# A hybrid decoder layer on one core: the opening rebuilt around a transposed x

## The chip, the cores and the metric

The kernel runs on one core of one Trainium2 chip. The core has a tensor engine (PE, with its weight loads listed as PEld), a vector engine (DVE), a scalar engine (ACT), GpSimd (POOL) and SyncE (SP), which issues nearly all DMAs here. The metric is the device time of one execution in microseconds; lower is better.

## The reference, cut to what matters

One layer is computed for a prompt of 1024 tokens and a group of 8 x 8 sample tokens, 1088 tokens of width 1024 together. Only the first steps matter for this change:

```python
shift, scale, gate = split(silu(c) @ ada_w + ada_b, 3)      # one set for the prompt, one for each of 8 samples
h = rmsnorm(x, norm_w) * (1 + scale) + shift
q_lat, kv_lat, k_pe, g_a, u, g_b, m_a, m_b = split_in(h @ w_in)
...
x = x + gate * (merged @ w_out)
```

`rmsnorm` divides each token by the root of the mean of its 1024 squares. `u` (512 columns) feeds a causal convolution and a recurrence; the other columns feed latent attention (prompt and paged sample attention), gates and mixers. `gate` is needed only at the end.

## The kernel before, in words

Tokens are cut into three groups, `GRP = [(0, 364), (364, 362), (726, 362)]`; the last holds the 64 sample tokens. The 1024 features are `KC = 8` chunks of 128. A product in high precision is three f32r products (`mm3`: high by high, high by low, low by high), so each operand is split by `split` into a rounded copy (ACT) and the remainder (DVE).

The opening is the block with the pools `p1`, `pj1`, `pt1`, `px1`. PE's instructions there keep the order of the program; those of the other engines and of the DMA queue are placed by a planner, which also moves an instruction ahead of earlier ones if its inputs are there.

- `x_load` brings nine tiles of 128 tokens by 1024 features. `x_norm` sums a tile's squares on ACT, takes the power -0.5 on GpSimd (`rms_pow`) and scales the tile on DVE or GpSimd. `x_turn` turns it on PE (eight transposes) and copies it out of PSUM to `xT`, feature by token.
- `ada_load`, `ada_sum`, `ada_turn` make shift and scale of one feature chunk: a 1 MB load (`aw`), eight products with 32 columns of weights that use four column strips of PE, a copy (`sa`), two transposes (`padt`), then three small DVE instructions that leave `aff`.
- `h_part` makes h of one chunk and group: an affine instruction on GpSimd (two DVE instructions for the samples), then `split` into `hh` and `hl`.
- `u_part` multiplies a chunk into the first two column tiles of `u`: six f32r products for one group, 18 for a chunk. The loop over k runs `u_part` for chunk k, and between its groups `ada_turn` and `h_part` of chunk k + 1 and `ada_sum` of chunk k + 2.

Then `u_evac` copies the u tiles to `L[0]` and `L[1]`, whose buffers the split u weights held.

After the opening, `dense` runs through 24 further column tiles of `w_in` (`project`: 24 products of three for a tile and group). `interleave` and `sample_attention` mix it with the recurrence and with sample attention by a clock `clk` that adds up estimated PE times. In its sixteen tiles from the third on, `beside` also carries one turn of `gate_sums`: a load of 256 KB, four f32 products with 32 columns of weights (`pada`), and a copy or add into `sgs`, the tile that holds the gate's partial sums until the last stage.

## Time and profile before

| | us |
|---|---|
| median of 3 runs (lowest to highest) | 973.25 (972.82 to 973.26) |
| the profiled execution | 971.41 |
| its span | 969.6 |
| PE busy in the span | 936.1 |
| first u product starts | 28.32 |
| first projection of `dense` starts | 66.41 |

The span runs from the first instruction to the last, and lies 1.8 us under the profiled execution's own time. Times in the trace count from the span's start. PE's busy time counts pipelined products that overlap, so pitches (start to start) say more than durations.

### The profile page before, as it was taken

To read this page: it belongs to the slowest core of one execution; us is meant where nothing else is said; L and a number is where in the kernel's file an instruction comes from. 1 tells how busy PE (TensorE), PEld (TensorE's weight loads), DVE (VectorE), ACT (ScalarE), POOL (GpSimd) and SP (SyncE) were. 2 spreads that over 40 slices of the span, in tenths; PEclk is the share of its full clock that TensorE was granted. 3 is DMA by queue.
4 is the path that set the end of the run, shared out by engine and by line. 5 is a ranking of instruction groups with operands and counts; after the bars stand their busy time and mean duration, and the time that the engine had idled before them with its cause. 6 is when DMAs were issued, how large, how long until landed. Compare 5 with 4: busy or idle time off the path is not lost. (4 is left out here: it accounts for less than half of the span.)

```text
span 969.6 us, 16493 instructions
## 1 busy us (share of the span) xinstructions
PE 936.1 (97%) x5933; PEld 860.2 (89%) x5933; DVE 645.5 (67%) x1518; ACT 492.2 (51%) x1150; POOL 241.0 (25%) x313
## 2 busy tenths in 40 slices
PE   5899999999999999999999999999999899999997
PEld 4677999999999999999999898888888799998886
DVE  5775664566666777766654367889889785880833
ACT  6447555544445444544443336777687664650311
POOL 5452210332222322222100034444445200000101
PEclk9999999999999999999999999999999999999999
DMA  9843132453443323333422213000011264741421
GB/s 337 287 142 110 49 108 94 146 152 109 141 129 125 113 77 120 103 110 119 117 78 97 65 53 69 12 7 22 7 34 34 69 198 155 246 140 35 152 87 66
DMA packets 52099, 104.62 MB, mean 108 GB/s; under 512 B 8177, under 2 KB 23601, under 8 KB 50994
## 3 DMA queue, kind: packets, MB, share of 16 engines
q1 hardware_dynamic: 46626, 84.69, 26.8%
q0 software_dynamic: 5392, 18.88, 6.6%
q8 instruction: 47, 0.77, 0.3%
q14 instruction: 34, 0.28, 0.1%
HBM read 85.58 MB, written 16.92 MB: 106 GB/s over the span
## 5 line engine op out<-in xcount | busy, mean ns | idle before, releaser
L79 PE MATMUL pj<-hh,whi 128*128 128x362 f32 (+2 forms) x656 | 223.9, 341 | 1.1 <-ACT L L145 1.1
L81 PE MATMUL pj<-hh,wlo 128*128 128x362 f32 (+2 forms) x656 | 217.1, 331 | 0.0
L80 PE MATMUL pj<-hl,whi 128*128 128x362 f32 (+2 forms) x656 | 216.8, 330 | 0.0
L79 PEld LDWEIGHTS pj<-hh,whi 128*128 128x128 f32 x656 | 123.5, 188 | 7.5 <-issue 4.7
L80 PEld LDWEIGHTS pj<-hl,whi 128*128 128x128 f32 x656 | 123.7, 189 | 1.7 <-issue 0.4
L81 PEld LDWEIGHTS pj<-hh,wlo 128*128 128x128 f32 x656 | 123.4, 188 | 1.7 <-issue 0.4
L644 POOL TENSOR_SCALAR nat<-raw 128x1024 fp32r<-128x1024 f32 x32 | 37.0, 1157 | 136.6 <-PE spo L65 81.6
L1038 POOL TENSOR_SCALAR pr<-pr,mx 128x128 f32<-128x128 f32 (+3 forms) x64 | 50.0, 782 | 83.2 <-DVE mx L1037 69.3
L1036 ACT ACTIVATE pr<-pr,mx 128x128 f32<-128x128 f32 (+3 forms) x64 | 49.8, 778 | 12.9 <-DVE mx L1034 12.6
L645 DVE TENSOR_TENSOR nat<-raw,nat 128x1024 fp32r<-128x1024 f32 x32 | 39.0, 1220 | 20.6 <-POOL nat L644 20.6
L641 POOL DMA_INDIRECT raw<-cache_ckv,idx x32 | 33.6, 1049 | 74.9 <-PE ptt L69 44.4
L1052 PE MATMUL ptr<-ident,pr 128*128 128x128 f32 x288 | 45.6, 276 | 4.1 <-DVE ptl L56 2.7
L112 POOL TENSOR_SCALAR ost<-ost 128x1 f32<-128x1 f32 (+1 forms) x9 | 2.9, 324 | 186.0 <-DVE ost L1296 186.0
L1293 ACT ACTIVATE ot<-xo 128x512 f32<-128x512 f32 (+2 forms) x19 | 11.5, 606 | 72.8 <-DVE xo L1292 68.5
L56 DVE TENSOR_TENSOR ptl<-ptr,pth 128x512 fp32r<-128x512 f32 (+1 forms) x80 | 45.7, 577 | 3.6 <-ACT pth L55 2.4
L694 ACT COPY stmp<-pss 64x512 f32<-64x512 f32 (+1 forms) x40 | 19.9, 497 | 55.0 <-PE pss L65 54.7
L56 DVE TENSOR_TENSOR wlo<-wraw,whi 128x512 fp32r<-128x512 f32 x58 | 39.4, 703 | 10.1 <-ACT whi L55 10.0
L55 ACT CAST pth<-ptr 128x512 fp32r<-128x512 f32 (+1 forms) x80 | 39.6, 499 | 9.7 <-PE ptr L1052 9.1
L56 DVE TENSOR_TENSOR tt<-ptt,tt 128x512 fp32r<-128x512 f32 x64 | 41.2, 679 | 4.8 <-ACT tt L55 4.4
L1052 PEld LDWEIGHTS ptr<-ident,pr 128*128 128x128 f32 x288 | 33.0, 140 | 12.6 <-DVE ptl L56 3.9
L55 ACT CAST whi<-wraw 128x512 fp32r<-128x512 f32 x58 | 34.0, 621 | 13.5 <-PE pj L80 13.4
L345 DVE COPY ev<-pj 128x364 f32<-128x364 f32 (+1 forms) x40 | 21.2, 530 | 29.4 <-PE pj L81 28.9
(472 smaller groups left out, 2588.5 us busy)
## 6 DMA issues: line engine op xcount, KB each, us to landing
wraw<-w_in SPq DMA_DIRECT2D x60, 256.0 KB, 3.2
sg<-g_dram SPq DMA_DIRECT2D x16, 544.0 KB, 3.6
aw<-ada_ss SPq DMA_DIRECT2D x8, 1024.0 KB, 7.2
g_dram<-ev SPq DMA_DIRECT2D x40, 181.0 KB, 2.4
wraw<-ada_g SPq DMA_DIRECT2D x16, 256.0 KB, 3.0
oraw<-w_out SPq DMA_DIRECT2D x16, 256.0 KB, 3.2
xo<-xp SPq DMA_DIRECT2D x8, 512.0 KB, 5.3
out_y<-xo SPq DMA_DIRECT2D x16, 256.0 KB, 2.1
```

The costliest lines, as they stand in the source:

```text
L55: S.copy(hi, src)
L56: V.tensor_tensor(lo, src, f(hi), OP.subtract)
L79: T.matmul(out, lhs[0], rhs[0], start=start, stop=False)
L80: T.matmul(out, lhs[0], rhs[1], start=False, stop=False)
L81: T.matmul(out, lhs[1], rhs[0], start=False, stop=stop)
L345: (S.copy if g == 1 else V.tensor_copy)(ev[:, :n], ps[:, :n])
L641: nc.gpsimd.indirect_dma_start(raw.rearrange("p k r -> p (k r)"), None, ckv_rows, bass.IndirectOffsetOnAxis(ap=idx[:, j, b:b + 1], axis=0))
L644: G.tensor_scalar(nat[:, 0], raw, 1.0, 0.0, OP.mult, OP.add)
L645: V.tensor_tensor(nat[:, 1], raw, f(nat[:, 0]), OP.subtract)
L1036: S.activation(pr[:, :w], pr[:, :w], AF.Exp, bias=mx[:, 1:2], scale=-1.0, accum_out=mx[:, 2:3])
L1038: G.tensor_scalar(pr[:, :w], pr[:, :w], mx[:, 3:4], 0.0, OP.mult, OP.add)
L1052: T.transpose(ps[:, k, i, :], pr[i][:, kc * P:(kc + 1) * P], ident)
```

## The change: what it does

The host now also lays x out feature by token, as three arrays `xT0` to `xT2`, one for each token group. `x_load` brings each in two halves of four chunks. The squares are taken on ACT, chunk by chunk; DVE (groups 0 and 1) or GpSimd (group 2) adds the eight up; PE sums over the partitions with a column of ones; the power is taken for three columns at once; three diagonal tiles and a product with a matrix of ones spread the result over all partitions (`R`). DVE then scales x in place: the first two chunks in the opening, the others in `h_part`, where the sample instructions go to GpSimd. Eight warm-up products of the identity stand ahead of the first modulation sum. The loop turns the modulation two blocks ahead instead of one, and has four buffers `aw` instead of three. The gate's sums use `ada_sum` on four loads of 1 MB: two in the last blocks, two at the end of the opening. `gate_sums` and its turns in `beside` are removed. The diff, cut to its core:

```diff
-        G.tensor_tensor(out, tmp, nhalf[:n], OP.pow)
+        G.tensor_tensor(out, tmp, nhalf[:n].to_broadcast(tuple(out.shape)), OP.pow)
...
-            xT = p1.tile([P, KC, N], F32, name="xT", bufs=1)
+            xg = [p1.tile([P, KC, n], F32, name=f"xT{g}", bufs=1) for g, (_, n) in enumerate(GRP)]
+            ones = p1.tile([P, P], F32, name="ones", bufs=1)
+            V.memset(ones, 1.0)
             def ada_load(k):
-                aw = p1.tile([P, KC, 256], F32, name="aw", bufs=3)
-                nc.sync.dma_start(aw, a["ada_ss"][k])
+                aw = p1.tile([P, KC, 256], F32, name="aw", bufs=4)
+                nc.sync.dma_start(aw, a["ada_ss"][k] if k < KC else a["ada_g"][k - KC])
...
+            def x_load(g):
                 for j in range(2):
+                    nc.sync.dma_start(xg[g][:, 4 * j:4 * j + 4], a[f"xT{g}"][:, 4 * j:4 * j + 4])
+            def x_sum(g):
+                n = GRP[g][1]
+                acc = p1.tile([P, 364], F32, name="acc", bufs=3)
+                S.activation(acc[:, :n], xg[g][:, 0], AF.Square)
+                for k in range(1, KC):
+                    sq = p1.tile([P, 364], F32, name="sq", bufs=3)
+                    S.activation(sq[:, :n], xg[g][:, k], AF.Square)
+                    (V if g < 2 else G).tensor_tensor(acc[:, :n], acc[:, :n], sq[:, :n], OP.add)
+                return acc
+            def x_turn(g, acc):
+                pq = px.tile([P, 4], F32, name="pst", tag="px")
+                for i, m in cut[g]:
+                    T.matmul(pq[:m, i:i + 1], acc[:, i * P:i * P + m], ones[:, 0:1], start=True, stop=True)
...
+                V.tensor_copy(st[g][:, 0:2], pq[:, 0:2])
+                V.tensor_copy(st[g][:m, 2:3], pq[:m, 2:3])
+                rms_pow(st[g][:, 4:7], st[g][:, 0:3], D, st[g][:, 0:3])
+            def x_spread(g):
+                rinv = p1.tile([P, 3, P], F32, name="rinv", bufs=2)
+                for i in range(3):
+                    V.tensor_scalar(rinv[:, i], ident, st[g][:, 4 + i:5 + i], None, OP.mult)
+                ps = pt.tile([P, 512], F32, name="prb", tag="pt")
+                T.matmul(ps[:, :n], ones, rinv.rearrange("p i t -> p (i t)")[:, :n], start=True, stop=True)
+                R[g] = p1.tile([P, 364], F32, name=f"R{g}", bufs=1)
+                S.copy(R[g][:, :n], ps[:, :n])
+            def x_scale(g, k, m):
+                x = xg[g][:, k:k + m]
+                V.tensor_tensor(x, x, R[g][:, :n].rearrange("p t -> p () t").to_broadcast((P, m, n)), OP.mult)
             def h_part(k, g):
...
+                if k > 1:
+                    x_scale(g, k, 1)
                 if s + n > NP:
...
-                    V.tensor_tensor(h3, xT[:, k, NP:]..., OP.mult)
-                    V.tensor_tensor(h3, h3, aff[:, k, 0, 1:9]..., OP.add)
+                    G.tensor_tensor(h3, x3, aff[:, k, 1, 1:9]..., OP.mult)
+                    G.tensor_tensor(h3, h3, aff[:, k, 0, 1:9]..., OP.add)
                     split(hh[k][:, NP:], hl[k][:, NP:], hs[:, k])
+                G.tensor_scalar(h[:, s:m], x[:, :m - s], aff[:, k, 1, 0:1], aff[:, k, 0, 0:1], OP.mult, OP.add)
                 split(hh[k][:, s:m], hl[k][:, s:m], h[:, s:m])
+            def gate_sum(j):
+                return ada_sum(aw[KC + j], sgs[:, 256 * j:256 * j + 256])
...
+            for g in range(3):
+                x_load(g)
+            aw = {0: ada_load(0)}
+            u01 = [weights(a["w_in"][c], (0,), (w_u0, None)[c]) for c in range(2)]
+            aw[1], aw[2] = ada_load(1), ada_load(2)
+            for c in range(2):
+                weights(a["w_in"][c], (1,), u01[c])
+            aw[3] = ada_load(3)
+            for g in range(3):
+                x_turn(g, x_sum(g))
+                x_spread(g)
+                x_scale(g, 0, 2)
+            warm = px.tile([P, P], F32, name="warm", tag="px")
             for i in range(8):
+                T.matmul(warm, ident, ident, start=i == 0, stop=i == 7)
+            sa = ada_sum(aw[0])
+            aw[4] = ada_load(4)
+            ada_turn(0, sa)
+            for g in range(3):
+                h_part(0, g)
+            sa = ada_sum(aw[1])
+            aw[5] = ada_load(5)
+            def block_sum(k):
+                if k < KC:
+                    r = ada_sum(aw[k])
+                elif k < KC + 2:
+                    r = gate_sum(k - KC)
+                if k + 4 < KC + 4:
+                    aw[k + 4] = ada_load(k + 4)
+                return r
+            def block_turn(k, sa):
+                if k < KC:
+                    ada_turn(k, sa)
+                    for g in range(3):
+                        h_part(k, g)
             for k in range(KC):
                 if k == 3:
                     w_u2 = weights(a["w_in"][2])
+                u_part(k, 0)
+                if k == 0:
+                    block_turn(1, sa)
+                    u_part(0, 1)
+                    sa = block_sum(2)
+                    u_part(0, 2)
+                    block_turn(2, sa)
+                else:
+                    sa = block_sum(k + 2)
+                    u_part(k, 1)
+                    block_turn(k + 2, sa)
+                    u_part(k, 2)
+            gate_sum(2)
+            gate_sum(3)
+            nc.sync.dma_start(sgs[9:10], a["gate_b"])
...
             def beside(n):
                 w[n + 1] = weights(a["w_in"][tiles[n + 1][0] if n + 1 < len(tiles) else 8])
-                m = n - 2
-                sums = gate_sums(m // 2, m % 2) if 0 <= m < 16 else iter(())
-                next(sums, None)
-                yield
-                next(sums, None)
                 yield
```

## Rows read from the trace of the kernel before

**Rows 1.** The page, busy time, share and instructions of each engine.

```profile
PE 936.1 (97%) x5933; PEld 860.2 (89%) x5933; DVE 645.5 (67%) x1518; ACT 492.2 (51%) x1150; POOL 241.0 (25%) x313
```

**Rows 2.** Windows of the opening: length, busy time by engine, PE's clock, DMA, GB/s.

```profile
10.00:12.00 2.00, 2.00 (x10) 1.64 (x9) 0.15 (x1) 1.77 (x4) 1.74 (x4) 1.00 1.03 422
...
30.00:31.00 1.00, 1.00 (x6) 0.92 (x5) 0.41 (x2) 0.60 (x3) 0.00 (x0) 0.50 0.70 279
...
33.00:34.00 1.00, 1.00 (x18) 0.50 (x11) 1.00 (x3) 0.66 (x2) 1.00 (x1) 1.00 0.10 41
```

**Rows 3.** Timeline from 7 to 18 us: start, length, instruction, idle before it.

```profile
7.49 0.21 POOL L532 COPY L<-vec 128x24 f32<-128x24 f32 x1
...
8.74 1.06 ACT L224 ACTIVATE L<-x 128x1024 f32<-128x1024 f32 x1 [0.32 <-DMA x<-xp]
...
9.04 6.99 PE L238 MATMUL pxt<-ident,x 128*128 128x128 f32 x32 [9.04 <-DVE x L229]
...
14.59 0.19 POOL L112 TENSOR_SCALAR st<-st 128x1 f32<-128x1 f32 x1
...
14.86 0.55 POOL L113 TENSOR_TENSOR st<-st,nhalf 128x1 f32<-128x1 f32 x1
...
16.34 1.07 PE L238 MATMUL pxt<-ident,x 128*128 128x128 f32 x8 [0.31 <-DVE x L229]
```

**Rows 4.** Timeline of PE in the u stage and into the first projection.

```profile
28.32 0.43 PE L79 MATMUL pu<-hh,wuh 128*128 128x364 f32 x1 [2.38 <-ACT hh L55]
...
40.21 0.33 PE L81 MATMUL pu<-hh,wlo 128*128 128x364 f32 x1
40.38 0.39 PE L202 MATMUL padt<-ident,sa 128*128 128x128 f32 x2
...
40.77 0.33 PE L80 MATMUL pu<-hl,wuh 128*128 128x362 f32 x1
...
41.43 0.32 PE L81 MATMUL pu<-hh,wlo 128*128 128x362 f32 x1
41.69 1.07 PE L194 MATMUL pada<-aw,sc 128*32 128x256 f32 x16
...
42.96 0.33 PE L80 MATMUL pu<-hl,wuh 128*128 128x362 f32 x1
...
59.13 0.38 PE L202 MATMUL padt<-ident,sa 128*128 128x128 f32 x2
...
61.70 0.43 PE L79 MATMUL pu<-hh,wuh 128*128 128x364 f32 x1 [0.20 <-ACT hh L55]
...
66.41 0.43 PE L79 MATMUL pj<-hh,whi 128*128 128x364 f32 x1 [1.06 <-ACT L L145]
```

**Rows 5.** PE around the first gate turn; then all turns of that tile.

```profile
118.94 0.33 PE L81 MATMUL pj<-hh,wlo 128*128 128x362 f32 x1
119.20 0.42 PE L65 MATMUL pada<-wraw,sc 128*32 128x128 f32 x8
...
119.83 0.33 PE L80 MATMUL pj<-hl,whi 128*128 128x362 f32 x1
...
L65 PE MATMUL pada<-wraw,sc x128: 272/285/297, 119.2 to 385.2; 128*32 128x128 f32 x128
```

**Rows 6.** GpSimd's instructions by shape: count, busy time, mean ns, idle before.

```profile
L937 POOL TENSOR_TENSOR csr<-csr,sq 128x512 f32<-128x512 f32 x2 | 2.6, 1280 | 64.4 <-ACT sq L908 64.4
...
L1295 POOL TENSOR_TENSOR xo<-xo,gain 128x256 f32<-128x256 f32 x1 | 0.7, 739 | 0.9 <-ACT ot L1293 0.9
```

**Rows 7.** Timelines of GpSimd and DVE in one block of the u stage.

```profile
42.36 0.64 POOL L245 TENSOR_SCALAR L<-xT,aff 128x362 f32<-128x362 f32 x1
42.93 0.54 DVE L56 TENSOR_TENSOR hl<-L,hh 128x364 fp32r<-128x364 f32 x1 [0.91 <-ACT hh L55]
42.99 0.95 POOL L245 TENSOR_SCALAR L<-xT,aff 128x298 f32<-128x298 f32 x1
```

**Rows 8.** Timeline of PE at a product in plain f32 (ones by squares).

```profile
567.93 1.02 PE L938 MATMUL qss<-csr,ones 128*128 128x512 f32 x2
```

More of the change, by code (lines that the diff above doesn't have):

```diff
@@ L194, in ada_sum @@
                     T.matmul(ps[32 * t:32 * t + 32, :], sc[:, j, :], aw[:, j, :], start=j < 4, stop=j >= 4)
-                sa = p1.tile([P, 256], F32, name="sa")
+                sa = p1.tile([P, 256], F32, name="sa") if sa is None else sa
                 S.copy(sa, ps)
@@ L231, in x_turn @@
-            def x_turn(i):
-                n, x = P if i < 8 else NS, xs[i]
-                for j in range(2):
-                    ps, tag = ((pt, "pt"), (pj, "pj"), (pj, "pj"))[(2 * i + j) % 3]
-                    ps = ps.tile([P, 4, P], F32, name="pxt", tag=tag)
-                    for k in range(4):
-                        T.transpose(ps[:, k, :n], x[:n, (4 * j + k) * P:(4 * j + k + 1) * P], ident[:n, :n])
-                    (S.copy if j == 0 and i % 2 == 0 else V.tensor_copy)(xT[:, 4 * j:4 * j + 4, i * P:i * P + n], ps[:, :, :n])
@@ L255, in trunk_step, with u_part @@
             pu = {}
[L257 removed]
+            def u_part(k, g):
                 s, n = GRP[g]
[L259 to L279 removed]
@@ L280, in trunk_step @@
-            aw = ada_load(2)
-            h_part(0, *GRP[0])
-            h_part(0, *GRP[1])
-            h_part(0, *GRP[2])
-            sa = ada_sum(aw1)
-            for k in range(KC):
-                if 0 < k and k + 2 < KC:
-                    aw = ada_load(k + 2)
-                if k == 0:
-                    for c in range(2):
-                        weights(a["w_in"][c], (1,), u01[c])
+                for c in range(2):
+                    if k == 0:
+                        pu[c, g] = (pj if g < 2 else pt).tile([P, 512], F32, name=f"pu{c}{g}",
+                                                             tag="pj" if g < 2 else "pt")
+                    mm3(pu[c, g][:, :n], [w[:, k, :] for w in u01[c]], [hh[k][:, s:s + n], hl[k][:, s:s + n]],
+                        k == 0, k == KC - 1)
@@ new lines, in trunk_step @@
+            for g in range(3):
[3 more added lines that the diff above has]
+            aw[1], aw[2] = ada_load(1), ada_load(2)
+            for c in range(2):
+                weights(a["w_in"][c], (1,), u01[c])
[5 more added lines that the diff above has]
+            warm = px.tile([P, P], F32, name="warm", tag="px")
@@ L324, in project @@
                 next(beside, None)
-        def gate_sums(k, q):
-            aw = wp.tile([P, 512], F32, name="wraw", bufs=3)
-            nc.sync.dma_start(aw.rearrange("p (k j) -> p k j", k=4), a["ada_g"][k, :, 4 * q:4 * q + 4])
-            yield
-            ps = pj.tile([P, P], F32, name="pada", tag="pj")
-            for t in range(4):
-                mm(ps[32 * t:32 * t + 32, :], sc[:, 4 * q + t, :], aw[:, P * t:P * t + P], start=True, stop=True)
-            to = sgs[:, P * k:P * k + P]
-            if q == 0:
-                V.tensor_copy(to, ps)
-            else:
-                V.tensor_tensor(to, to, ps, OP.add)
-            if k == 7 and q == 1:
-                nc.sync.dma_start(sgs[9:10], a["gate_b"])
         def spill(c):
```

75 lines of the change are left out of this document (20 added, 55 removed).

## The prediction

> **What bounds the kernel now.** The page's engine totals come first: the tensor engine (PE) is busy for 97% of the span [rows 1], so what it must execute, and when it can begin, sets the end. The windows and the timeline then divide the part that the change touches in two. From 0 to 28.3 us PE only turns x and waits; its first u product starts at 28.32, the first projection of the next stage at 66.41, and from there PE runs with few holes until the end [rows 4]. So the sum needs three numbers: when the first u product starts, how long the u stage lasts, and what the sixteen gate turns cost among the projections.
>
> The clock column belongs beside it. It stands at 0.50 (1.2 GHz) in the microsecond from 30, after 2.38 us without work ahead of 28.32, and at 1.00 (2.4 GHz) in that from 33 [rows 2, 4]. The column also says 1.00 in the first microseconds, but there 32 transposes take 6.99 us, 0.218 each, and later eight take 1.07, at most 0.134 each [rows 3]: PE starts slow there too and comes up only after several microseconds of work.
>
> **What leaves the projections.** In each of the sixteen places PE goes from the product before a gate turn to the second after it in 0.89 us (118.94 to 119.83); two ordinary products take 0.333, so a turn costs 0.555 [rows 5]. PE does not wait there, so nothing hides it: 16 x 0.555 = -8.9 us. Their copies and adds on the vector engine (DVE) and their 256 KB loads are off the path and are priced at nothing.
>
> **What the u stage becomes.** It holds 144 u products. At 2.4 GHz their pitch is 0.1665. A modulation sum put between them costs 1.53 - 0.333 = 1.197 (41.43 to 42.96), a turn 0.56 - 0.333 = 0.23 (40.21 to 40.77) [rows 4]. After the change: 144 x 0.1665 = 24.0; eight sums between products (2 to 7, and two of the gate) 9.6; seven turns 1.6; the last two gate sums back to back 2 x 1.07 = 2.1, which also cover the 1.06 that PE now waits for the evacuation before 66.41. Together 37.3. Before, the stage took 66.41 - 28.32 = 38.1, with the slow clock and some stalls in it; because the turns come a block earlier I take most stalls as gone and leave 0.7 for new ones (0 to 3): 38.0, a difference of -0.1. If the clock fell again as it did before 30 it would cost some 1.5 more.
>
> **When the first u product starts.** PE's program order is fixed, so the summed squares of the third token group, their turn, the spread, eight warm-up products and the first modulation sum all stand ahead of it. Backwards from there:
>
> - Arrival. The third x tile (1.91 MB moved, the three constant tables included) was there at 8.74, when its square began [rows 3]. The first half of the third group ends at 4.05 MB; the rest goes at 422 GB/s [rows 2]: 8.74 + 5.1 = 13.8. Two squares of 364 columns (0.38 each by columns from 1.06 for 1024 [rows 3]) and their latency put GpSimd's first add at 14.7.
> - Seven adds on GpSimd. A two-input instruction takes 1.28 at 512 columns and 0.739 at 256 [rows 6], so 0.97 at 362: 6.8 us. The second group's power stands in the same queue: 0.19 + 0.55 for one column [rows 3], 0.36 of it for the power; three columns cost between 0.85, hops included, and 1.6; I take 1.0. End without disturbance: 22.5.
> - Collisions. GpSimd needs 0.64 for 362 columns alone, but 0.95 for 298 when a two-input DVE instruction started just before it [rows 7]: 0.42 is lost by one collision (0.53 would be due). While the adds run, DVE has the eight scalings of the first group, ready as soon as its spread is: an instruction that is ready is placed early here even if its stage comes much later (the copy of line 532 at 7.49 belongs to the recurrence [rows 3]). Eight collisions: 3.4 (0 if they fall elsewhere, 5 with the weight splits and a part of the second group's scalings). End: 25.9.
> - Turn of the third group: six short passes on PE at the low clock, 0.2 each as the transposes [rows 3], 1.2; two copies 0.45; the power 1.0; three diagonal products on DVE 0.65 (0.22 each, an estimate by the columns of 0.54 for 364 [rows 7]): 3.3.
> - Spread. A product of 512 columns in plain f32 comes in two passes that take 1.02 together, 0.43 apart [rows 8], so 0.61 for 362 at 2.4 GHz. PE has done almost nothing until here, so I take 1.2 GHz: 1.25.
> - Warm-up. Eight times 128 columns are two such products: 1.7 at the high level, 3.4 at the low one. PE came up only after more than 3.4 us of work in both places that the trace shows (from 28.32 to after 31, and the transposes from 9.04), so I take 3.4.
> - First modulation sum: 1.07 at the high level [rows 4], about 1.9 at the low; 1.5. Copy from PSUM 0.45. From a turn's start to the u product that needs its features: 59.13 to 61.70, 2.57 [rows 4].
>
> 25.9 + 3.3 + 1.25 + 3.4 + 1.5 + 0.45 + 2.57 = 38.4, against 28.3: +10.1.
>
> **The sum.** -8.9 - 0.1 + 10.1 = +1.1. The profiled execution took 971.41, so 972.5 for one like it; it lies 1.84 below the median of 973.25, so 974.3 in those terms. The new opening gives back almost exactly what the projections gain. Differences within 0.2% (1.95 us) are about what a measurement of this kernel can't tell from no change.
>
> Edits at no cost: the loads of the gate weights (four of 1 MB; each is issued four sums before it is used, some 18 us by the blocks above, and takes 2.5 us at 422 GB/s [rows 2]); the two sample instructions of each block that go to GpSimd; the new layout on the host. The 72 transposes of x and their copies save nothing by themselves: they end in 28.3, which the chain above replaces.
>
> A sentence from the notes beside it: the Trainium skill (GPSIMD Engine Reference, 3.1 Elementwise) gives 4497 ns for a two-input add of 2048 columns. By that the seven adds take 5.6 us, an estimate from that page, not 6.8, and the sum would be 973.1. The trace's own rows at 256 and 512 columns are nearer in size.
>
> **Rivals.**
>
> *The start is hardly late (faster).* If the scalings fall after GpSimd's adds and the clock rises in the middle of the warm-up, 3.4 and 1.2 go away: -3.5, 969.8. For it: nothing but the order that the planner finds puts the scalings early, and the program names them only at the blocks that use them. Against it: the early copy at 7.49, and adds that run for 7 us while DVE has free time. It decides when the adds end before 22.8.
>
> *The shared port bounds the blocks (slower).* If the scalings for features 2 to 7 are not made early, each block holds on DVE three scalings and four subtractions with two inputs (about 2.6 us at 0.42 for 364 columns) and on GpSimd three affine instructions (1.8) and the two sample ones (0.3 each, between the 0.19 and 0.55 of its short instructions [rows 3]): 5.0, and 5.6 if each scaling also waits 0.2 for GpSimd as the second subtraction of a block does now. PE's block is 18 x 0.1665 + 1.2 + 0.23 = 4.4. Six blocks lose 7.1, less 1.5 of lead; the early collisions (3.4) and the 0.3 of stalls already counted go away: 1.1 + 5.6 - 3.7 = +3.0, 976.3. It becomes slower than before by more than 0.2% from 5.4 us a block on. For it: in the rows the two engines take turns rather than overlap [rows 7]. Against it: DVE has idle time between the third group's spread and the first u product, some 9 us, for just these scalings. The Trainium skill (GPSIMD Engine Reference, 1. Specifications) states that GpSimd's SBUF interface is shared with the vector engine and contended by its two-input instructions; by that rule it is this rival that happens, at 976.3, and the trace's 0.95 against 0.53 agrees.
>
> *The gain in the projections doesn't arrive.* If something else ended those stretches, only the late start would be left: 983. PE's uninterrupted pitch on both sides of each turn speaks against it.
>
> **Chances.** No change within 0.2% (971.3 to 975.2): 0.38, where the likeliest sum, 974.3, lies. Faster: 0.27, the first rival and shorter GpSimd adds. Slower: 0.35, of which the shared port 0.2, the third rival 0.02, and the upper ends (powers of three columns at 1.6 twice, +1.2; stalls up to 3; collisions up to 5) 0.13. The range takes the first rival at its lower end and the upper bounds added to the sum, +5.2: 969.5 to 979.5.
>
> **What the next profile would show.** Right: the first u product between 36 and 40; GpSimd's adds above 0.97 in the mean and ending near 26; warm-up products 0.43 apart; sums between u products at 1.2 and no `pada` among the projections; first projection 38 us after the first u product. Wrong if the adds end by 22, if the warm-up runs at the high clock from its start, if u blocks are longer than 4.6 with waits for the features, or if an engine's queue holds the third group's squares behind a copy of an earlier spread (ACT serves both), which would add up to 2 us.

## The result, and the profile after

The changed kernel takes 994.36 us (median of 4, 993.57 to 996.7), the kernel before beside it 973.04 (4 runs): a ratio of 1.0226, 95% interval 1.0213 to 1.0239. It is slower by 21 us where no change was forecast. The span is 992.7 against 969.6, so 23.1 us have to be found, of which the forecast had 1.1. Three marks on PE divide them: the first u product, the first projection, and the first product of squares behind the attention (`qss`).

| | before | forecast | after | after against forecast |
|---|---|---|---|---|
| first u product | 28.3 | 38.4 | 43.9 | +5.5 |
| length of the u stage | 38.1 | 38.0 | 48.3 | +10.3 |
| first projection to `qss` | 501.5 | 492.6 | 499.0 | +6.4 |
| from there to the end | 401.7 | 401.7 | 401.5 | -0.2 |

All three terms are off, in the same direction. PE's busy time, from the page, is what it was in [rows 1]; the time is lost in idle PE and at the low clock.

```profile
PE 934.9 (94%) x5837; PEld 859.7 (87%) x5837; DVE 649.9 (65%) x1522; ACT 493.2 (50%) x1158; POOL 241.2 (24%) x320
```

**The opening**, in timelines of ACT, DVE, GpSimd (POOL) and PE, answers to [rows 3] and [rows 6].

```profile
14.54 0.51 ACT L228 ACTIVATE sq<-xT 128x362 f32<-128x362 f32 x1 [1.77 <-DVE acc L229]
16.71 1.15 ACT L228 ACTIVATE sq<-xT 128x362 f32<-128x362 f32 x2 [1.66 <-DVE st L238]
17.90 0.46 ACT L253 COPY R<-prb 128x364 f32<-128x364 f32 x1
...
13.70 0.16 DVE L239 COPY st<-pst 128x2 f32<-128x2 f32 x1 [1.20 <-PE pst L236]
15.55 0.68 DVE L249 TENSOR_SCALAR rinv<-ident,st 128x128 f32<-128x128 f32 x3 [1.04 <-POOL st L113]
25.45 2.05 DVE L249 TENSOR_SCALAR rinv<-ident,st 128x128 f32<-128x128 f32 x3 [1.04 <-POOL st L113]
...
19.64 3.45 POOL L229 TENSOR_TENSOR acc<-acc,sq 128x362 f32<-128x362 f32 x3 [4.12 <-ACT sq L228]
24.54 0.87 POOL L113 TENSOR_TENSOR st<-st,nhalf 128x3 f32<-128x3 f32 x1
25.38 4.57 POOL L229 TENSOR_TENSOR acc<-acc,sq 128x362 f32<-128x362 f32 x4
...
30.00 1.37 PE L236 MATMUL pst<-ones,acc 128*128 128x1 f32 x6 [0.88 <-POOL acc L229]
35.28 3.22 PE L310 MATMUL warm<-ident 128*128 128x128 f32 x16
38.43 1.07 PE L198 MATMUL pada<-aw,sc 128*32 128x256 f32 x16
39.99 0.44 PE L206 MATMUL padt<-ident,sa 128*128 128x128 f32 x2 [0.49 <-ACT sa L200]
43.90 0.43 PE L79 MATMUL pu<-hh,wuh 128*128 128x364 f32 x1 [2.47 <-ACT hh L55]
```

GpSimd's first add stands at 19.64, not at 14.7. The reason stands one engine further up. ACT makes the squares in order and stops twice for 1.7 us, because its three buffers are freed by adds on DVE, and DVE's queue holds the first group's turn ahead of the second group's adds: the copy at 13.70 waits for PE, the diagonal products at 15.55 wait for the power. (The view puts the second stop down to `st`, a tiny DVE instruction at 16.62; the add that frees the buffer ended beside it, at 16.68.) Behind that ACT copies the first spread (17.90) before it squares the third group.

**The u stage**, answer to [rows 4] and [rows 7]: one block in timelines of PE, GpSimd and ACT.

```profile
58.41 0.44 PE L206 MATMUL padt<-ident,sa 128*128 128x128 f32 x2 [1.68 <-ACT sa L200]
60.78 1.07 PE L198 MATMUL pada<-aw,sc 128*32 128x256 f32 x16
63.80 0.44 PE L206 MATMUL padt<-ident,sa 128*128 128x128 f32 x2 [0.76 <-ACT sa L200]
...
59.76 1.27 POOL L278 TENSOR_SCALAR L<-xT,aff 128x364 f32<-128x364 f32 x2 [2.29 <-DVE aff L210]
61.00 0.66 POOL L273 TENSOR_TENSOR hs<-xT,aff 128x64 f32<-128x64 f32 x1
61.65 0.95 POOL L278 TENSOR_SCALAR L<-xT,aff 128x298 f32<-128x298 f32 x1
62.57 0.29 POOL L275 TENSOR_TENSOR hs<-hs,aff 128x64 f32<-128x64 f32 x1
...
62.89 0.25 ACT L55 CAST hh<-hs 128x64 fp32r<-128x64 f32 x1 [1.33 <-POOL hs L275]
63.05 0.43 ACT L55 CAST hh<-L 128x298 fp32r<-128x298 f32 x1
63.39 0.36 ACT L200 COPY sa<-pada 128x256 f32<-128x256 f32 x1
```

This is a closed loop. The turn at 58.41 gives the affine numbers; GpSimd works on them until 62.86; ACT's casts of its last results run until 63.5; only behind them in ACT's queue, at 63.39, comes the copy of a sum that PE had ended at 61.85; and the next turn, at 63.80, waits for that copy. From 53.10 to 74.43 a turn comes every 5.3 us. In the kernel before, the turn at 40.38 [rows 4] was followed by one at 44.79, 4.41 later; lines of its timelines of ACT and PE:

```profile
44.32 0.37 ACT L196 COPY sa<-pada 128x256 f32<-128x256 f32 x1
...
44.79 0.39 PE L202 MATMUL padt<-ident,sa 128*128 128x128 f32 x2
```

There the copy ended 0.1 us ahead of the turn that needed it, and PE did not wait. In the changed kernel 0.95 of the loop are the two instructions on `hs` that the change put on GpSimd. The view of PE's waits in the stage sums it up (total, times, longest), and below it a window of the changed kernel, answering to [rows 2], shows the low clock at the stage's start (0.50 in the third column from the right):

```profile
PE padt L206 <- ACT sa L200: 8.0, 6, 2.6
```

```profile
46.00:48.00 2.00, 2.00 (x9) 0.50 0.11 37
```

**The projections.** No `pada` stands among them any more, as it did in [rows 5]. The view of SP's waits, the timelines of SP, GpSimd and PE, and windows of PE show what does:

```profile
SPq L352 <- ACT sgs L200: 8.8, 1, 8.8
```

```profile
93.30 0.30 SPq L352 DMA_DIRECT2D sgs<-gate_b  x1
94.63 1.33 SPq L482 DMA_DIRECT2D kqr<-w_kvq  x3
...
115.05 2.58 POOL L595 TENSOR_TENSOR gi<-gi,uc 128x1112 f32<-128x1112 f32 x1 [1.08 <-ACT gi L590]
117.71 0.19 POOL L112 TENSOR_SCALAR kst<-kst 64x1 f32<-64x1 f32 x1
118.26 0.55 POOL L113 TENSOR_TENSOR kst<-kst,nhalf 64x1 f32<-64x1 f32 x1
...
119.24 0.27 PE L69 MATMUL pqt<-ident,kvsq 64*128 64x64 f32 x1 [2.58 <-DVE kvsq L508]
```

```profile
120.00:122.00 2.00, 2.00 (x8) 0.50 0.00 0
```

The load of the gate's bias (line 352, one row) waits 8.8 us at the head of SP's queue for the copy of the last gate sum. Behind it stand the weights of the sample queries (`kqr`), issued 2.4 us after the first projection (92.21); in the kernel before they were issued at 62.7, 3.7 us ahead of it. SP's and GpSimd's timelines of the kernel before:

```profile
62.71 1.28 SPq L452 DMA_DIRECT2D kqr<-w_kvq  x3
...
86.73 0.55 POOL L113 TENSOR_TENSOR kst<-kst,nhalf 64x1 f32<-64x1 f32 x1
87.72 2.58 POOL L565 TENSOR_TENSOR gi<-gi,uc 128x1112 f32<-128x1112 f32 x1 [0.44 <-ACT gi L560]
```

There the queries' power stands ahead of a product of 2.58 us on GpSimd. In the changed kernel the queries come later, their power lands behind that product, PE waits 2.58 for the result (`kvsq`), and works at the low clock behind that wait. Over the whole stretch PE's waits are 5.9 us against 3.6 before, and the windows of 10 us with a clock below 1.00 (0.88, 0.95, and 0.89, 0.94 from 542) cost 3.4 us against none: together 5.7 of the 6.4 that are missing. Half of the 3.4 lies in the first two of these windows, behind the wait for `kvsq`.

### The profile page after: what moved, and what is told of

It reads as the page before. It is cut to its first block, busy times and chain, and to the rows that moved or that the text cites. A ratio compares the mean times of both kernels' runs of the same rounds, so it can differ in the third digit from the quotient of the medians.

```text
span 992.7 us, 16330 instructions
## 1 busy us (share of the span) xinstructions
PE 934.9 (94%) x5837; PEld 859.7 (87%) x5837; DVE 649.9 (65%) x1522; ACT 493.2 (50%) x1158; POOL 241.2 (24%) x320
## 5 line engine op out<-in xcount | busy, mean ns | idle before, releaser
L674 POOL TENSOR_SCALAR nat<-raw 128x1024 fp32r<-128x1024 f32 x32 | 34.8, 1088 | 135.2 <-PE spo L65 66.5
L671 POOL DMA_INDIRECT raw<-cache_ckv,idx x32 | 31.6, 987 | 76.0 <-PE ptt L69 58.4
L79 PE MATMUL pout<-woh,mgh 128*128 128x512 f32 (+1 forms) x102 | 38.4, 377 | 0.0
```

What stands on the lines that cost most here:

```text
L79: T.matmul(out, lhs[0], rhs[0], start=start, stop=False)
L671: nc.gpsimd.indirect_dma_start(raw.rearrange("p k r -> p (k r)"), None, ckv_rows, bass.IndirectOffsetOnAxis(ap=idx[:, j, b:b + 1], axis=0))
L674: G.tensor_scalar(nat[:, 0], raw, 1.0, 0.0, OP.mult, OP.add)
```

## The experiments

First all of them beside one another; ratios are to the kernel before on the same chip. The three marks are read from the one execution that was profiled; it took 998.51 in e3 and 986.42 in e13, the longest execution of each, and 972.35 in e4, the shortest.

| run | first u | first projection | `qss` | median | ratio, 95% interval |
|---|---|---|---|---|---|
| after | 43.9 | 92.2 | 591.2 | 994.36 | 1.0226 (1.0213 to 1.0239) |
| e1_sample_on_dve | 43.9 | 86.1 | 586.2 | 989.58 | 1.0184 (1.0166 to 1.0202) |
| e2_no_warm | 41.4 | 91.7 | 593.1 | 996.32 | 1.0246 (1.0226 to 1.0265) |
| e3_sums_first | 42.7 | 91.1 | 595.2 | 994.07 | 1.0221 (1.0208 to 1.0234) |
| e4_gates_moved_only | 28.5 | 69.5 | 568.9 | 974.62 | 1.0036 (1.0021 to 1.0051) |
| e5_gates_moved_bias_late | 29.0 | 71.7 | 566.8 | 969.38 | 0.9969 (0.9957 to 0.9981) |
| e6_after_bias_late | 44.7 | 93.1 | 590.4 | 993.69 | 1.0203 (1.0184 to 1.0222) |
| e7_adds_on_dve | 46.0 | 92.8 | 591.1 | 996.0 | 1.0248 (1.0231 to 1.0264) |
| e8_squares_free | 47.9 | 94.4 | 593.8 | 997.58 | 1.0261 (1.024 to 1.0282) |
| e11_one_turn | 43.6 | 93.5 | 593.2 | 997.54 | 1.0271 (1.025 to 1.0292) |
| e12_three_mended | 42.6 | 86.9 | 582.8 | 985.66 | 1.0137 (1.012 to 1.0154) |
| e13_mended_no_warm | 41.7 | 86.9 | 583.3 | 982.92 | 1.0112 (1.0096 to 1.0129) |
| e14_two_turns | 42.9 | 95.3 | 597.0 | 999.27 | 1.0272 (1.0257 to 1.0288) |
| e15_copy_on_dve | 43.5 | 93.9 | 593.8 | 997.86 | 1.0272 (1.0252 to 1.0292) |
| e16_loop_open | 44.8 | 89.1 | 583.2 | 986.83 | 1.0157 (1.0137 to 1.0176) |
| e17_sample_and_bias | 43.2 | 85.4 | 580.8 | 985.36 | 1.0146 (1.0122 to 1.017) |

### Where the gate sums' gain went

e4: the kernel before, with the gate sums alone moved.

```diff
-                    if k + 2 < KC and g == 1:
-                        sa = ada_sum(aw)
+                    if g == 1:
+                        j = k + 2 - KC
+                        sa = ada_sum(aw, sgs[:, 256 * j:256 * j + 256] if j >= 0 else None)
...
+            for j in (2, 3):
+                ada_sum(aw[j - 2], sgs[:, 256 * j:256 * j + 256])
+            nc.sync.dma_start(sgs[9:10], a["gate_b"])
...
-                m = n - 2
-                sums = gate_sums(m // 2, m % 2) if 0 <= m < 16 else iter(())
-                next(sums, None)
-                yield
-                next(sums, None)
```

> The kernel before with one part of the change alone: the gate sums leave the projections (sixteen turns of 0.555 there) and stand as four sums in the u stage and at its end, in the layout of the change; x, its squares and its transposes as before. Theory A: the projections gain all of 8.9 us when nothing else shifts, the four sums cost 2 x 1.2 + 2.1 less the 1.06 that PE waited for the evacuation: 3.5. So 973.0 becomes 967.5 to 969. Rival B: the stall of 2.6 us that after shows at 119 us (the power of the key-value norm behind a product of 2.58 us on GpSimd, then the low clock for some microseconds) comes from the projections being shorter; it appears here too and the time is 971.5 to 973.5.

Measured: the u stage takes 41.0, 2.9 more, and the projections 499.4, only 2.1 less; 974.62, slower than before (interval 1.0021 to 1.0051). The wait for `kvsq` is here too, without any of the new opening; from the view of PE's waits:

```profile
PE pqt L69 <- DVE kvsq L463: 2.6, 1, 2.6
```

This is rival B's stall, then, though the time lies above the 971.5 to 973.5 that it gave; its cause is not shown yet. e5 takes e4 and moves one load of one row:

```diff
-            nc.sync.dma_start(sgs[9:10], a["gate_b"])
...
                 w[n + 1] = weights(...)
+                if n == 17:
+                    nc.sync.dma_start(sgs[9:10], a["gate_b"])
```

> The run that moved the gate sums alone, with one more edit: the load of the gate's bias into row 9 of the gate sums leaves the end of the u stage and is issued in the projection of tile 17, about where the kernel before has it. Theory A: at the end of the u stage that load waits at the head of SP's queue for the copy of the last gate sum (8.8 us in the trace of after, until 93.30), and all loads behind it with it, those of the sample queries' weights above all; these are issued at 94.6 in after, 2.4 us behind the first projection, where before they were issued 3.7 ahead of it. So the planner puts the queries some 6 us later, their power lands behind the long product on GpSimd (2.58), and PE waits 2.6 and then runs slow for some microseconds. With the load later the queries come back to 21 us behind the first projection, the wait for kvsq falls below 1, and the span falls from 970.6 to 963.5 to 967; median 966 to 969. Rival B: the planner's order shifts for another reason (the modulation loads of 1 MB ahead of it on the queue); then the wait of 2.6 stays and the time within 1.5 us of 974.6.

Measured: 969.38 against 974.62, 5.2 us by the medians for this load, and 495.1 against 499.4 for the stretch from the first projection to `qss`; faster than before by 0.3%, interval 0.9957 to 0.9981. SP's and GpSimd's timelines of e5:

```profile
71.73 1.33 SPq L438 DMA_DIRECT2D kqr<-w_kvq  x3
...
94.42 0.55 POOL L113 TENSOR_TENSOR kst<-kst,nhalf 64x1 f32<-64x1 f32 x1
96.28 2.60 POOL L551 TENSOR_TENSOR gi<-gi,uc 128x1112 f32<-128x1112 f32 x1 [1.31 <-ACT gi L546]
```

The power now stands ahead of the long product, as in the kernel before, and PE's wait for `kvsq` is gone. Three points of theory A missed: the median lies 0.4 above its range, the queries come 24 us behind the first projection, not 21, and the span (968.4) stays above 967, as PE waits for the queries' weights (1.7 us) and the cache (1.3), with a stretch at the low clock. The u stage takes 42.7, against 41.0 in e4, with a wait of 1.4 for a load of gate weights in it (0.5 in e4) and more of it at the low clock (0.93 against 0.96 in the mean).

The same load in the changed kernel (e6), and there together with the edit of e1 below (e17):

> The changed kernel with the load of the gate's bias issued in the projection of tile 17 and nothing else. Theory A (that load holds SP's queue, and so the weights of the sample queries, until the u stage has ended): the wait of 2.6 us for kvsq at 119 us and the slow clock behind it go, the stretch from the first projection to qss falls from 499.0 to 493 to 496, and 994.4 becomes 988.5 to 992. Rival B (other loads on that queue are what is late): the stretch stays at 498 to 500.

> The changed kernel with the sample instructions on the vector engine and the load of the gate's bias in the projection of tile 17; the opening as in after. If the loop and the queue are two causes, each with a price of its own, the u stage is near 42.2 as in the run with the first edit alone, the stretch from the first projection to qss 495 to 497.5, and the time 984 to 987. If the time is 989 or more, the second edit brings nothing on top of the first.

Measured: in e6 the wait for `kvsq` and the low clock behind it go, but the clock falls at 542 to 562 instead (0.74 and 0.92 in windows of 10 us, after 0.89 and 0.94), and the time hardly moves: 993.69, a miss for A's size, with a stretch of 497.3 that lies below rival B's 498 to 500 too. Two of its five executions took 990.3 and 990.8, within A's range; the profiled one was not among them. In e17, where no window of the projections is below 1.00, the stretch takes 495.4 (e1: 500.1), as expected, and the time falls by 4.2 against e1, where the two intervals just touch. So the load's price in the stretch is 4.3 (e4, e5) and 4.7 us (e1, e17) in two of three pairs; in the third it is 1.7, as the low clock came at another place.

### What lengthened the blocks

e1 puts the two sample instructions back on DVE:

```diff
-                    G.tensor_tensor(h3, x3, aff[:, k, 1, 1:9]..., OP.mult)
-                    G.tensor_tensor(h3, h3, aff[:, k, 0, 1:9]..., OP.add)
+                    V.tensor_tensor(h3, x3, aff[:, k, 1, 1:9]..., OP.mult)
+                    V.tensor_tensor(h3, h3, aff[:, k, 0, 1:9]..., OP.add)
```

> The changed kernel with one thing undone: the two sample instructions of each feature block (the product and the sum of h3) stand on the vector engine again, as before the change. Theory A: the u blocks take 5.31 us (turns of the modulation at 53.10, 58.41, 63.80, 69.11, 74.43) because a loop runs through GpSimd's queue: turn, affine numbers, three affine instructions and these two on GpSimd, the casts on ACT, and behind them ACT's copy of the next sum, which the next turn waits for. With the two gone from GpSimd (0.3 to 0.66 each in the trace of after) the block falls to 4.4 to 4.6 and the u stage from 48.3 to 42 to 44: 994.4 becomes 988 to 990. Rival B: the blocks are set by the shared port of the vector engine and GpSimd (scalings, subtractions and affine instructions take turns); then the two instructions cost as much on the vector engine, the block stays above 5.1 and the time within 2 us of 994.4. Neither expects a change ahead of 43.90 or in the projections.

Measured: the u stage falls from 48.3 to 42.2, the time to 989.58. Turns on PE's timeline:

```profile
60.48 0.39 PE L206 MATMUL padt<-ident,sa 128*128 128x128 f32 x2
64.90 0.39 PE L206 MATMUL padt<-ident,sa 128*128 128x128 f32 x2
```

This block takes 4.42 us and PE doesn't wait: theory A. Three of the stage's seven blocks take 4.4 to 4.5 us, the other four 5.0 to 5.6. The waits for the copy fall from 8.0 to 1.8 in that stage. Which link of the loop matters, ACT's queue or GpSimd's own work, is e15's question: the copy goes to DVE, the sample instructions stay on GpSimd.

```diff
-                S.copy(sa, ps)
+                V.tensor_copy(sa, ps)
```

> The changed kernel with the copy of each modulation sum from PSUM on the vector engine instead of ACT, and the sample instructions left on GpSimd. Theory A (the loop): in after each turn waits for this copy (8.5 us in all), which stands in ACT's queue behind the casts of the block before, and these wait for GpSimd's last instruction; on the vector engine the copy doesn't wait for the casts, the loop is open, GpSimd's own work of a block (three affine instructions and two sample ones, 2.9 to 3.6 us) is below PE's 4.4, so the blocks fall from 5.31 to 4.4 to 4.7 and the u stage from 48.3 to 42 to 44: 988 to 990. Rival B: GpSimd's work in a block is the bound, not the queue order; then the turns are no longer late but the u products wait for their features, and the block stays above 5.1. Rival C: on the vector engine the copy stands behind subtractions that wait for the same casts; block and time as in after.

Measured: rival C. Behind three turns without a wait come blocks of 9.3, 6.0, 5.9 and 6.9 us; the u stage takes 50.4, the time is 997.86. DVE's and PE's timelines:

```profile
62.80 0.47 DVE L56 TENSOR_TENSOR hl<-L,hh 128x298 fp32r<-128x298 f32 x1
63.19 0.42 DVE L200 COPY sa<-pada 128x256 f32<-128x256 f32 x1
...
63.66 0.44 PE L206 MATMUL padt<-ident,sa 128*128 128x128 f32 x2 [4.27 <-DVE sa L200]
```

PE had ended that sum at 58.2. On DVE its copy stands behind the subtraction, which stands behind the same casts: the loop is longer by a link. Either engine's order closes it, so e15 does not part the two links. The trace of after does: GpSimd is idle for 2.29 us before each block's work (59.76 above), until the affine numbers come, so it has time left and the order is what binds. e16 makes the edits of e15, e1 and e6 together:

> The changed kernel with the copy of the sums and the sample instructions on the vector engine, and the load of the gate's bias in the projection of tile 17. If the loop is what lengthened the blocks, the u stage comes to 40 to 42.5 (39.6 to 41 by 38.0 with the slow clock at its start and no waits for the copy); with the projections at 495 to 498, 983 to 986.5. Rival: the vector engine becomes the bound of a block (scalings, subtractions, the two sample instructions and the copy); the u stage stays above 43 and the time above 987.

Measured: u stage 44.2, 986.83: against e17, which has the copy on ACT (42.2 and 985.36), the copy on DVE costs 2.0 us of the stage; the intervals of the two times overlap. The expectation was a miss; with the sample instructions gone from GpSimd, ACT is the better place for the stage.

### What sets the start

Five kernels were made to bring the third group's adds forward. e3 puts the sums of all groups ahead in program order:

```diff
+            accs = [x_sum(g) for g in range(3)]
             for g in range(3):
-                x_turn(g, x_sum(g))
+                x_turn(g, accs[g])
```

> The changed kernel with the program order of the opening changed: the squares and their adds of all three token groups stand ahead of the first group's turn, spread and scaling. Theory A: the third group's squares come late (first add on GpSimd at 19.64 where 14.7 was forecast) because the vector engine's queue holds the first group's turn ahead of the second group's adds (idle 1.20 and 1.04 there) and the three square buffers then stop ACT. With the sums first, GpSimd's first add falls to 15 to 17, its last ends at 24.5 to 27 instead of 29.95, and the first u product comes 3 to 5 us earlier: 994.4 becomes 989 to 991.5. Rival B: GpSimd's adds are bound by collisions with the vector engine; then they begin earlier but get longer (above 1.2 in the mean) and the start moves by under 1.5 us. Rival C: the adds are released by the loads; then the first add stays near 19.6 and nothing moves.

Measured: the planner puts nearly the same order into the queues; first add 19.91, first u product 42.7, 994.07. It tested little. e7 puts the third group's adds on DVE, e8 frees the squares (first line pair e7, the rest e8):

```diff
-                    (V if g < 2 else G).tensor_tensor(acc[:, :n], acc[:, :n], sq[:, :n], OP.add)
+                    V.tensor_tensor(acc[:, :n], acc[:, :n], sq[:, :n], OP.add)
...
-                aw = p1.tile([P, KC, 256], F32, name="aw", bufs=4)
+                aw = p1.tile([P, KC, 256], F32, name="aw", bufs=3)
...
-                    sq = p1.tile([P, 364], F32, name="sq", bufs=3)
+                    sq = p1.tile([P, 364], F32, name="sq", bufs=8)
...
-                S.copy(R[g][:, :n], ps[:, :n])
+                V.tensor_copy(R[g][:, :n], ps[:, :n])
```

> The changed kernel with the third group's seven adds on the vector engine instead of GpSimd. Theory A: the late end of these adds (29.95 us where 25.9 was forecast) comes as much from when the squares are made (first add at 19.64) as from GpSimd's 1.15 us for each; on the vector engine one takes 0.45 to 0.53, so the seven end at 23.5 to 26 and the first u product comes at 38 to 40.5 instead of 43.90; the time 989 to 991.5. Rival B: the vector engine is full there (scalings, diagonal products), the adds queue behind these and end above 28; the first u product stays above 42.

> The changed kernel with eight buffers for the squares instead of three (room for them from the modulation weights, three buffers instead of four) and the copy of each spread on the vector engine, so that ACT's squares wait neither for adds nor for a copy. GpSimd keeps its seven adds. The u stage changes with the modulation weights, so the first u product is what counts here. Theory A: ACT's in-order queue and the three buffers made the third group late; now its squares begin at 14.5 to 16, GpSimd's first add stands at 15 to 16.5, its last ends at 24 to 26.5, and the first u product at 38 to 40.5. Rival B: GpSimd's adds themselves are the limit, stretched by the vector engine's two-input instructions; they start earlier but take 1.3 or more, end above 27.5, and the first u product is above 41.

Measured: both miss. In e7 the adds end at 30.9, one by one between scalings on DVE, and the first u product comes at 46.0. In e8 the buffers and the copy together bring the first add forward, as the account of the late add has it, and it doesn't help. GpSimd's timeline:

```profile
15.41 2.03 POOL L229 TENSOR_TENSOR acc<-acc,sq 128x362 f32<-128x362 f32 x2
25.14 0.85 POOL L112 TENSOR_SCALAR st<-st 128x3 f32<-128x3 f32 x1 [4.34 <-DVE st L241]
27.82 2.03 POOL L229 TENSOR_TENSOR acc<-acc,sq 128x362 f32<-128x362 f32 x2
```

The adds begin at 15.41 and four are done by 20.8; then the second group's power, next in GpSimd's queue, waits 4.34 us for a copy on DVE, and the last adds end at 29.85 as in after. The third group's turn then stands on PE behind the second group's spread, at 31.35, and its power begins at 34.8 (32.2 in after), so the first u product comes at 47.9. e11 takes the turns out of the queues: one set of 1-column products, one power over nine columns, from which each spread takes its three; the calls:

```diff
...
-            for g in range(3):
-                x_turn(g, x_sum(g))
-                x_spread(g)
-                x_scale(g, 0, 2)
+            st = x_turn([x_sum(g) for g in range(3)])
+            for g in range(3):
+                x_spread(g, st)
+                x_scale(g, 0, 2)
```

> The changed kernel with one turn of the sums for all three token groups: all squares and adds first, then one set of 1-column products, one power over nine columns on GpSimd, and then the three spreads. Nothing else is changed; GpSimd keeps the third group's adds. Theory A: the opening is late because the turn, spread and scaling of the first two groups stand in the in-order queues of ACT, the vector engine and GpSimd ahead of the third group's squares and adds, and because the scalings collide with the adds. Without them ACT squares from 6.8 to 17.5 us without a stop, GpSimd's seven adds take 0.95 to 1.0 each from 14.5 to 16 on and end at 21.5 to 23.5 (29.95 in after), and the first u product comes at 36.5 to 39.5 instead of 43.90, although PE then does three spreads in a row (3.1 to 4.7). The time falls from 994.4 to 988 to 991. Rival B: GpSimd's adds or the squares are slow by themselves; the last add ends above 26 and the first u product above 41. Rival C: the start comes earlier but PE runs at the low clock for longer behind it, so that the first projection moves by under 3 us.

Measured: seven adds without a stop, and 5.5 us earlier; GpSimd's and PE's timelines:

```profile
16.90 7.49 POOL L229 TENSOR_TENSOR acc<-acc,sq 128x362 f32<-128x362 f32 x7 [15.60 <-ACT sq L228]
26.54 1.82 POOL L113 TENSOR_TENSOR st<-st,nhalf 128x9 f32<-128x9 f32 x1
...
24.45 1.37 PE L238 MATMUL pst<-ones,acc 128*128 128x1 f32 x6 [5.60 <-POOL acc L229]
33.82 1.54 PE L257 MATMUL prb<-rinv,ones 128*128 128x362 f32 x2 [1.91 <-DVE rinv L255]
43.56 0.43 PE L79 MATMUL pu<-hh,wuh 128*128 128x364 f32 x1 [2.34 <-ACT hh L55]
```

But the first u product is at 43.56: the last turn starts at 24.45, and 19.1 us lie behind it instead of 13.9, with the power over nine columns (1.82 against 0.87), all three spreads, and diagonal products that wait. The time rises to 997.54. None of the three expectations came: the adds ended a little above A's range and well below B's, and the start did not move. e14 turns two groups together and the third alone; the calls again:

```diff
...
-            for g in range(3):
-                x_turn(g, x_sum(g))
-                x_spread(g)
-                x_scale(g, 0, 2)
+            for gs in ((0, 1), (2,)):
+                st = x_turn(gs)
+                for g in gs:
+                    x_spread(g, st)
+                    x_scale(g, 0, 2)
```

> The changed kernel with two turns of the sums instead of three: the first two token groups are summed and then turned together (one power over six columns), the third alone. In the run with one turn the adds ended 5.5 us earlier, at 24.4, but three spreads and a power over nine columns then stood between them and the first u product, which stayed at 43.6. Theory A: the start is set by what stands in a row behind the last add and by the turns that stand in the queues ahead of it; here only one spread and a power over three columns stand behind (13.9 us from the last add to the first u product in after), and only one turn stands ahead. The first add comes at 16.9, the last ends at 25.5 to 27.5, the first u product at 39 to 41.5 instead of 43.90, and the time is 989.5 to 992.5. Rival B: the wait moves again (the joint power and its copies hold GpSimd's adds, or the scalings hold the last turn): the adds end above 28.5 and the first u product stays at 42.5 to 45. Rival C: the start moves as in A and the clock takes it back in the u stage, so that the time stays within 2 us of 994.4.

Measured: the adds end at 27.4, in theory A's range, but the first u product comes at 42.9, in rival B's. The last turn starts at 27.48 (30.00 in after) and 15.4 us lie behind it. The time has the highest median of all, 999.27, as the u stage takes 52.4 and waits three times for the copy of a sum, up to 4.0.

The rest is the warm-up and the sum of the mends. e2 takes the eight products out, e12 joins the edits of e11, e6 and e1, e13 takes the warm-up out of e12 by the diff of e2:

```diff
-            warm = px.tile([P, P], F32, name="warm", tag="px")
-            for i in range(8):
-                T.matmul(warm, ident, ident, start=i == 0, stop=i == 7)
```

> The changed kernel without the eight warm-up products. In the trace of after they take 3.2 us from 35.28 (16 passes 0.21 apart, the low clock's pitch), the clock is at 1.00 behind them, and falls to 0.50 at 45 to 48 all the same. Theory A: they buy nothing that lasts; without them the first sum starts at 35.3, runs at the low clock (1.9 instead of 1.07), and the first u product comes 2.4 us earlier, at 41.5, with the blocks as they were: 994.4 becomes 991.5 to 992.5. Rival B: they do raise the clock for the first blocks; without them the low clock lasts longer into the u stage, the first u product comes 2.4 earlier, and the first projection at the same time or later: 994 to 997.

> Three edits together on the changed kernel: one turn for the three groups, the load of the gate's bias in the projection of tile 17, and the two sample instructions of each block on the vector engine. By theory A the three causes are in different stretches and add up: the first u product at 36.5 to 39.5, the u stage 41.5 to 43.5 long, 495 to 498 from the first projection to qss: 976 to 983 in all, within 1.2% of before and still slower, as the start stays 8 to 11 us later than before. Rival B: they are one queue of work that only moves; then the sum falls by less than 8 from 994.4.

> The run with the three edits, and without the eight warm-up products as well. Theory A: the three spreads in a row raise the clock for the first sum by themselves, so the warm-up only delays: the first u product comes 1.7 to 3.4 us earlier and the first projection 1 to 3. Rival B (as the run without warm-up alone showed): what the start gains is lost to a lower clock in the u stage; first projection within 1 us.

Measured: without the warm-up the first u product comes 2.5 earlier (e2) and the first projection at 91.7: rival B. Windows of e2 at the start of its u stage (clock in the third column from the right):

```profile
42.00:44.00 2.00, 1.87 (x6) 0.50 1.02 414
44.00:46.00 2.00, 1.75 (x7) 0.50 0.09 37
```

PE is at the low level from its first u products on. The time, 996.32, has an interval that overlaps the one of after, so what the warm-up is worth in all is not shown. e12 comes to 985.66, above the range of theory A: its one turn gains nothing over e17. e13 has the same first projection as e12 (86.9), as rival B says, yet a median 2.7 lower, with intervals that overlap; its marks are those of its longest execution, and that difference is left open.

## Why the prediction was wrong

**"Nothing hides it: 16 x 0.555 = -8.9 us", and "Edits at no cost: the loads of the gate weights".** The second step failed, and ate the first. The prediction priced four loads of 1 MB and passed over the fifth one that moves with them, the bias. It is small, but it waits for the last gate sum, in an in-order queue, ahead of the queries' weights. e4 and e5 differ by it alone, by 4.3 us of the stretch, e1 and e17 by 4.7; after and e6 by 1.7 only. In after the wait of 2.6 and the 1.7 lost at the low clock behind it are 4.3 of the 6.4; the 1.7 lost from 542 on have no cause that a run shows. The four loads of 1 MB were not quite free either: PE waited 1.4 for one of them in e5. The turns' own price fits: e5's 495.1, less 0.4 of waits more than before and 1.7 at the low clock, is 493.0 where 492.6 was forecast. The rival "the gain in the projections doesn't arrive" was given 2 in 100; it was most of what happened there.

**"I take most stalls as gone and leave 0.7".** This step failed by the largest amount. The sum of products, sums and turns was right: 37.3, plus 8.0 of waits for the copy and 1.9 at the low clock (0.96 over 48.3), is 47.2 of the measured 48.3; the last two gate sums took 1.93 together and covered the evacuation as said. What was missed is the loop. The kernel before has it too, at 4.41, the pace of PE itself (44.32 and 44.79 above): it had next to no slack for two more instructions on GpSimd, priced at nothing under "edits at no cost". Turning two blocks ahead does not open it, as each turn still waits behind the casts of the block before. e1 shows the price: 6.1 us of the stage. The 1.9 at the low clock the prediction had named, at 1.5, and left out of its sum.

**The shared port** was forecast as a rival with blocks of 5.0 to 5.6, and the block measures 5.3; but this is a coincidence. It needed scalings inside the blocks, and 20 of the 21 scalings on DVE were done by 42.8; and in e1, with the two sample instructions on DVE, blocks of 4.42 are back.

**"GpSimd's first add at 14.7".** It stood at 19.64. From there the working held: to the last add 10.3 against 11.2 forecast, from the last turn to the warm-up 5.3 against 4.6 (the spread's product took 1.55, not the 1.25 worked out from [rows 8]), the warm-up 3.2 at the low clock against 3.4, the first sum 1.07 against 1.5, from the turn to the u product 3.9 against 2.6, where GpSimd's first affine instruction took 1.72 beside scalings on DVE. The collisions on the adds were too high a term: the seven took 8.0 us in all, against 7.5 in e11, where DVE has no scalings, so 0.5 us and not 3.4 (by the medians, 1.12 and 0.95 each, 1.2). The second group's power and the wait ahead of it took 2.3 between them, not 1.0. In-order queues were named as something that could make the start late, by up to 2 us; it was 4.9, since DVE's queue did it as well as ACT's. The Trainium skill (Perfetto Trace Analysis, Tensor Engine Instruction) says that ACT, DVE and GpSimd take their instructions strictly in order; the wait of 4.34 in e8 agrees, and so does that of 1.20 in after (13.70 on DVE), with adds behind it whose squares were there.

**What stays open.** No single wait sets the start: adds that began 4.2 us earlier (e8) or ended 5.5 earlier (e11) left it between 43.6 and 47.9, each time for another reason that the timelines name. That a quicker opening of this form exists was not shown. Nor is it settled why the low clock comes at 542 to 562 in some of these kernels.

**The better version.** e5, the gate sums moved with the bias load left late, beats both kernels: 0.9969 of before. Beside e17, which has the new opening with the other two steps mended, it also shows about what that opening costs: the first u product at 43.2 against 29.0, and medians 16 us apart.

## What to carry to other kernels

When a step is moved, list every load that it issues, small ones too, with what each waits for and what is queued behind it: a load of one row that waits for the end of a stage makes all later loads of its queue wait for it. Before an instruction goes to an engine with idle time, follow the loop that runs through it, queue by queue, to its own next turn; if that loop's period is already PE's, the engine has no room for it. In a chain of turns over in-order queues, curing the wait that the trace names first mostly shows the next one, so ask what stands behind the last turn before rebuilding what stands ahead.

## What the runs showed of the hardware

A power on GpSimd costs by the column: 0.55 us for one column of 64 rows, 0.87 for three of 128, 1.35 for six (e14), 1.82 for nine (e11). An add of two inputs of 362 columns takes 0.95 there with DVE quiet. The Trainium skill (GPSIMD Engine Reference, 3.1 Elementwise) gives 4497 ns for 2048 columns, which is 0.80 for 362 by columns, an estimate; the measured add is longer. Collisions reach instructions with one tensor input as well: three diagonal products on DVE took 0.68 with GpSimd idle and 2.05 beside its adds (15.55 and 25.45 above; 2.05 again in e8, from 27.88). And the same short waits go with a low clock in one run and not in another: in after PE waited 0.58 and 0.18 us at 547 and ran at 0.83 over the 10 us from 550; in e17 it waited 1.00 and 0.18 before the same two products, at 538, and stayed at 1.00 from there to 562.
